# Reciprocal norms through TensorE to DRAM, first weight sums on VectorE, GpSimd multiplying before it splits: three moves in a one-core decoder block

## The chip, the cores and the metric

One core of a Trainium2 chip runs the whole block. The metric is device time in microseconds (us) of one execution, as a median over runs; all times in the sections on the profile come from one profiled execution. The engines are PE (TensorE), DVE (VectorE), ACT (ScalarE), POOL (GpSimd) and SP (SyncE, which issues most DMAs).

## The reference

One layer over 1024 tokens of width 1024, in float32, cut to what matters here:

```python
xn = rmsnorm(h, norm_mix_g)                 # row norms: y = x * rsqrt(mean(x*x) + eps)
proj = xn @ w_in                            # q, k, v, u, vg and one forget gate for each of 8 heads
att = forgetting_attention(q, k, v, log_sigmoid(proj[..., G_END:] + b_forget))
u, vg = gelu(proj_u), gelu(proj_vg)
mixed = einsum('gij,bnjgd->bnigd', tril(w_s), rmsnorm(vg)) + b_s     # 8 groups, chunks of 128
sg = u * mixed
h = h + concat([att, sg]) @ w_out
h = h + conv_ffn(rmsnorm(h)) @ ...          # w_up, causal convolution, silu gate, w_down
out = rmsnorm(h)
```

## The kernel before

Every float32 operand of a matmul is split into a high part (a cast to float32r) and a low part (the difference), and a product takes three matmuls: high by high, high by low, low by high. `tsplit` and `split_w` do this for weights (cast on ACT, difference on DVE, unless told otherwise); the result lies in a ring of six buffers (`wy`, `wy`, `whl` four times), so a cast waits until PE has read what the buffer held six splits ago. The projections are done as Strassen products over 2x2 blocks (in Winograd's form: sums S1 to S4 of weight blocks, T1 to T4 of x blocks).

The parts that the change touches, in the order of the program:

- **Row norms.** `rstd1` (128 x 8, token on the partition) holds the reciprocal norms. Products whose result has tokens on the partition use it as a per-partition scale. For k, whose result has tokens along the free axis, the norms must lie along the free axis on every partition: the kernel writes `rstd1` to DRAM (`rbd`, L411 to L413, a DMA on ACT's queue that stores 1024 single floats in transposed order) and reads it back broadcast into `rb` (L548, L549). `emit` multiplies k by `rb` (L625).
- **Weight sums of the q and k products.** `Weights(i)` loads four 128 x 512 blocks; `sums` and `last_sum` add them on POOL (L534, L537, L538, L544) for all four i. The sum S2 is then split, and its product is the third of the stage (`qk_step`). The products themselves are line L512: `q1` into bank `qc`, then `q2` into `qa`, then `qb`, `qc`, `qd`.
- **The forget gate.** The V products leave their last part in four PSUM banks `S2`. ACT copies 256 columns of each to SBUF (`copies`), and DVE adds 8 columns of each to `zf` (L562, recorded as L55). `q2` takes the first of these four banks, so its first matmul waits for both readers.
- **Gate normalisation.** `norm` multiplies half of the gated values by their reciprocal norms `gms` on DVE, 128 x 1024 at a time; `norm(1, 0)` and `norm(1, 2)` stand in front of the `zf` additions.
- **Spatial gating.** `spatial` runs eight groups g. The first half of the tokens is finished on DVE; of the second half ACT adds the bias into `t` and POOL multiplies `u[1]` by it (L808). PE then transposes both halves, `turn_sg(0, c)` and `turn_sg(1, c)` (L825), c from 0 to 3; the second needs POOL's products of groups 2c and 2c + 1.
- **Splits of the output weights.** `sg_split` splits four blocks `wrs`; for the first two the cast too is on POOL (L162), all four differences are (L166). They are used by `sg_out` (L1064 to L1066), which `fill` puts between the first attention logits (L976, L977) as filler for PE. DVE takes the row minimum of the logits (`logits_min`, L989).

ACT and DVE keep the order of the code in these stages (`Line` records it, and its operations have line L55 in the profile); where `on` is false, and for PE, POOL, SP and DMAs, a scheduler sets the order, with manual dependencies (`after`) for some.

## Time and profile before

| | |
|---|---|
| median of 3 runs | 1059.72 us (1059.09 to 1060.23) |
| profiled execution | 1062.91 us, of which the span of instructions is 1061.2 |
| PE busy | 1045.6 us, 99% of the span |
| DVE, ACT, POOL busy | 892.4, 564.7, 224.0 us |
| mean granted TensorE clock | 0.993 |
| HBM read and written | 115.68 and 45.05 MB |

Rows of a timeline give the start, the duration, the engine, the line, what is written and read, the count, and in brackets how long the engine was idle before and who ended that. Rows of a table by windows give, for each stretch, its length, then busy time and count for PE, PEld (weight loads), DVE, ACT and POOL, then the granted clock, the share of the DMA engines that was busy, and GB/s.

### The profile page before, as it was taken

How to read it: one execution, taken by the hardware profiler on the slowest of the kernel's cores; microseconds unless marked ns; L12 is line 12 of the kernel's file. 1: busy time of each engine (PE TensorE's matmuls, PEld its weight loads, DVE VectorE, ACT ScalarE, POOL GpSimd, SP SyncE). 2: the span in 40 equal slices, each digit the busy share in tenths (PEclk: the TensorE clock that was granted, in tenths of full speed). 3: DMA queues.
4: the chain of work that ended last, by engine and by line, in shares of the span. 5: the costliest groups of instructions: out<-in, count | busy, mean ns of one | idle time of the engine just before them, and what ended most of it. 6: DMA issues, size and time to landing. Idle time of an engine off the chain costs nothing.

```text
span 1061.2 us, 14270 instructions
## 1 busy us (share of the span) xinstructions
PE 1045.6 (99%) x4997; PEld 873.4 (82%) x4997; DVE 892.4 (84%) x1298; ACT 564.7 (53%) x1002; POOL 224.0 (21%) x169
## 2 busy tenths in 40 slices
PE   9999899989999999999999999999999999999997
PEld 6989788968888888888888888888888888888886
DVE  6897987858888869998999989989898866898775
ACT  6776533355777736654544444444444444544654
POOL 0001341220420740054333433323321000000000
PEclk9999999989999999999999999999999999999999
DMA  9624458848565445133245433332422899333442
GB/s 334 226 11 170 126 153 243 232 133 237 179 188 162 134 165 179 61 99 107 92 149 162 146 100 100 110 101 88 129 100 70 290 334 312 115 97 94 140 125 101
DMA packets 68475, 161.66 MB, mean 152 GB/s; under 512 B 9126, under 2 KB 10262, under 8 KB 68404
## 3 DMA queue, kind: packets, MB, share of 16 engines
q1 hardware_dynamic: 67092, 160.71, 48.0%
q8 instruction: 39, 0.64, 0.3%
q14 instruction: 32, 0.26, 0.1%
q10 hardware_dynamic: 1312, 0.04, 0.1%
HBM read 115.68 MB, written 45.05 MB: 151 GB/s over the span
## 4 chain that ended last, share of the span: by engine, by line
PE 82%; DVE 5%; ACT 3%; issue 1%; DMA 0%; POOL 0%; ACTq 0%; DVEq 0%; SPq 0%
PE k L1612 20%; PE qc L1352 11%; PE qd L1352 11%; PE qa L1352 10%; PE qb L1352 5%; PE pb L1040 3%; PE pb L1024 2%; PE qd L512 2%; PE qc L512 2%; PE qa L512 2%; PE ps L855 2%; PE pl L976 1%; PE pl L977 1%; PE pf L1064 1%; PE pf L1065 1%; PE pf L1066 1%
## 5 line engine op out<-in xcount | busy, mean ns | idle before, releaser
L1612 PE MATMUL k<-whb,wha 128*128 128x512 f32 (+1 forms) x936 | 209.9, 386 | 0.0
L1612 PEld LDWEIGHTS k<-whb,wha 128*128 128x128 f32 x936 | 174.1, 188 | 35.8 <-DVE wha L166 0.2
L1352 PE MATMUL qc<-xT,whb 128*128 128x512 f32 x540 | 129.9, 389 | 0.1
L1352 PE MATMUL qa<-xB,wha 128*128 128x512 f32 x528 | 127.4, 390 | 0.0
L1352 PEld LDWEIGHTS qc<-xT,whb 128*128 128x128 f32 x540 | 101.3, 188 | 21.6 <-ACT cg L1493 0.5
L1352 PEld LDWEIGHTS qa<-xB,wha 128*128 128x128 f32 x528 | 98.8, 188 | 20.8 <-DVE wha L166 0.4
L160 ACT CAST wha<-sg 128x512 fp32r<-128x512 f32 x77 | 47.8, 624 | 96.7 <-PE k L1612 84.1
L160 ACT CAST whb<-sg 128x512 fp32r<-128x512 f32 x82 | 50.7, 620 | 86.8 <-PE qc L1352 66.7
L166 DVE TENSOR_TENSOR wha<-sg,wha 128x512 fp32r<-128x512 f32 x77 | 52.8, 688 | 39.7 <-ACT wha L160 39.6
L1352 PE MATMUL qd<-xB,whb 128*128 128x512 f32 x264 | 63.7, 389 | 0.0
L1352 PE MATMUL qd<-xT,whb 128*128 128x512 f32 x264 | 63.7, 389 | 0.0
L1352 PE MATMUL qb<-xT,whb 128*128 128x512 f32 x252 | 61.0, 389 | 0.0
L166 DVE TENSOR_TENSOR whb<-sg,whb 128x512 fp32r<-128x512 f32 x82 | 57.0, 697 | 4.4 <-ACT whb L160 4.3
L1025 ACT CAST pt<-pb 128x512 fp32r<-128x512 f32 x72 | 40.6, 585 | 37.6 <-PE pb L1024 29.6
L1236 POOL TENSOR_TENSOR sg<-raw 128x512 f32<-128x512 f32 x20 | 31.1, 1553 | 139.7 <-DVE whb L166 79.9
L1352 PEld LDWEIGHTS qd<-xT,whb 128*128 128x128 f32 x264 | 49.5, 188 | 10.5 <-DVE u L1459 0.3
L1352 PEld LDWEIGHTS qd<-xB,whb 128*128 128x128 f32 x264 | 49.6, 188 | 10.3
L1026 DVE TENSOR_TENSOR pt<-pb,pt 128x512 fp32r<-128x512 f32 x72 | 47.3, 686 | 11.5 <-ACT pt L1025 11.2
L1352 PEld LDWEIGHTS qb<-xT,whb 128*128 128x128 f32 x252 | 47.2, 188 | 10.0 <-DVE whb L166 0.3
L1040 PE MATMUL pb<-pt,V 128*128 128x512 f32 (+3 forms) x192 | 49.6, 362 | 0.6 <-DVE pt L1026 0.6
L1239 POOL TENSOR_TENSOR sg<-sg,raw 128x512 f32<-128x512 f32 x20 | 33.3, 1663 | 63.5 <-DVE whb L166 63.5
L1237 POOL TENSOR_TENSOR sg<-sg,raw 128x512 f32<-128x512 f32 x20 | 35.1, 1756 | 47.2 <-issue 44.6
(409 smaller groups left out, 2259.8 us busy)
## 6 DMA issues: line engine op xcount, KB each, us to landing
raw<-wup SPq DMA_DIRECT2D x44, 512.0 KB
sg<-hx SPq DMA_DIRECT2D x77, 256.0 KB
hx<-hs SPq DMA_DIRECT2D x44, 256.0 KB
hx<-ca SPq DMA_DIRECT2D x35, 256.0 KB
xT<-wdn SPq DMA_DIRECT2D x28, 256.0 KB
x<-kd SPq DMA_DIRECT2D x24, 256.0 KB
A<-xtok SPq DMA_DIRECT2D x8, 512.0 KB
raw<-wqk SPq DMA_DIRECT2D x8, 512.0 KB
```

The costliest lines, as they stand in the source:

```text
L160: act.copy(h, src)
L166: return eng.tensor_tensor(out=l, in0=src, in1=f32(h), op=ALU.subtract)
L512: pe.matmul(ps, w[:, wi, ks], xs(n, xi, k), start=(first and c == 0), stop=(c == 11), skip_group_check=True)
L855: seq(pe.matmul(banks[m // 2][:, o:o + 256], xs(n, xi, 2 * j + kk)[:, ms], w[j][:, wi, kk * 256:kk * 256 + 256], start=(j == 0 and kk == 0 ...
L1025: casts.append(act.copy(pt[:, 0, :], ptr))
L1026: los.append(dve.tensor_tensor(out=pt[:, 1, :], in0=ptr, in1=f32(pt[:, 0, :]), op=ALU.subtract))
L1040: seq(pe.matmul(po[half][:, o:o + w], lhs, pt[:, s, c:c + w], start=(new and s == 0), stop=(s == 1 and (half, k) in ((1, 6), (0, 3))), ski ...
L1236: pool.tensor_tensor(out=s[0], in0=a21, in1=a22, op=ALU.add)
L1237: pool.tensor_tensor(out=s[1], in0=s[0], in1=a11, op=ALU.add)
L1239: pool.tensor_tensor(out=s[3], in0=s[1], in1=a12, op=ALU.add)
L1352: pe.matmul(ps, w[:, wi, ks], xb[:, xi, k, :], start=(first and n == 0), stop=(n == 11), skip_group_check=True)
L1612: pe.matmul((banks[bk + m] if ps is None else ps)[:, o], xh[:, xi, ms], wh[:, wi, o], start=((first and p_ == 0 or new) and n == 0), stop= ...
```

## The change

- `rstd1` is transposed by PE into unused columns of a PSUM bank, copied by ACT into the first 8 rows of `rb` (8 x 128), written to `rbd` as 8 rows of 128 floats by a DMA on SP's queue, and read back broadcast as before. The DMA on ACT's queue goes.
- For `Weights(0)` alone the four sums are done by DVE, between the splits; for i = 1, 2, 3 they stay on POOL.
- The split of S2 stands between `norm(1, 0)` and `norm(1, 2)`.
- POOL does the eight multiplications of `spatial` first, and then the splits of the output weights.

```diff
@@ after T4's products
-    act.on = False
-    act.dma_start(out=rbd.rearrange("a p -> p a"), in_=rstd1)
-    act.on = True
@@ before the products of S2's banks
+    pe.transpose(S[0][0:8, 384:512], rstd1, ident)
     S2 = [sbank() for _ in range(4)]
@@ class Weights
-        def sums(self, floor=None):
+        def sums(self, eng=pool, part=3):
...
+            if part & 2:
+                s2_ = sb("gg", [P, 512])
+                eng.tensor_tensor(out=a11, in0=a21, in1=a11, op=ALU.add)
+                eng.tensor_tensor(out=s2_, in0=a11, in1=a22, op=ALU.add)
+                self.src.update({"S3": a11, "S2": s2_})
+            if part & 1:
+                eng.tensor_tensor(out=a21, in0=a21, in1=a22, op=ALU.add)
+                self.src["S1"] = a21
...
     W = [Weights(0)]
-    rb = sb("t01", [P, 1024])
-    after(tc, sp.dma_start(out=rb, in_=rbd.rearrange("a b -> (a b)").unsqueeze(0).to_broadcast((P, 1024))), W[0].d)
     W[0].split("A11")
+    W[0].sums(dve, 2)
     act.activation(gms, gms, AF.Sqrt, bias=eps[:, 0:1], scale=1.0 / 64)
     dve.reciprocal(gms, gms)
     W[0].split("A12")
-    W[0].sums()
+    rb = sb("t01", [P, 1024])
+    act.copy(rb[0:8, 0:P], S[0][0:8, 384:512])
+    sp.dma_start(out=rbd, in_=rb[0:8, 0:P])
+    sp.dma_start(out=rb, in_=rbd.rearrange("a b -> (a b)").unsqueeze(0).to_broadcast((P, 1024)))
+    W[0].sums(dve, 1)
+    W[0].last_sum(dve)
     copies(S, vx[1], 1)
     norm(1, 0)
+    W[0].split("S2")
     norm(1, 2)
-    W[0].split("S2")
-    W[0].last_sum()
     copies(S2, vx[2])
@@ def sg_split
-        splits[:] = [split_w(wr, (w[:, 0], w[:, 1]), hi, "pool")]
+        if hi == "pool":
+            x = pool.tensor_copy(w[:, 0], wr)
+            after(tc, x, splits[0])
+            pool.tensor_tensor(out=w[:, 1], in0=wr, in1=f32(w[:, 0]), op=ALU.subtract)
+        else:
+            split_w(wr, (w[:, 0], w[:, 1]), hi, "pool")
@@ spatial, def second
-                x = pool.tensor_tensor(out=u[1], in0=v3(t), in1=u[1], op=ALU.mult)
-                after(tc, x, splits[0])
+                splits[:] = [pool.tensor_tensor(out=u[1], in0=v3(t), in1=u[1], op=ALU.mult)]
@@ ahead of spatial
-    for k in range(2):
-        whs.append(sg_split(wrs[k], "pool"))
@@ behind the first transposes
-    for k in range(2, 4):
-        whs.append(sg_split(wrs[k]))
+    for k in range(4):
+        whs.append(sg_split(wrs[k], "pool" if k < 2 else "act"))
```

DVE ahead of the gate additions, before: the splits of A11 and A12 (`whl` from `raw`), the two norms (`G` by `gms`), the split of S2 (`wy` from `gg`) and the first two additions to `zf`.

```order
L55 TENSOR_TENSOR whl_1065<-raw_1059,whl_1065 128x512
L55 RECIPROCAL gms<-gms 128x64
L55 TENSOR_TENSOR whl_1070<-raw_1059,whl_1070 128x512
L55 TENSOR_TENSOR G_187<-G_187,gms 128x1024 x2
L55 TENSOR_TENSOR wy_1089<-gg_1073,wy_1089 128x512
L55 TENSOR_TENSOR zf<-ps_1007,zf 128x8
L55 TENSOR_TENSOR zf<-ps_1008,zf 128x8
```

The same place on DVE after the change; `raw_1059` and `raw_1060` are the loaded weights, `gg_1066` is S2.

```order
L55 TENSOR_TENSOR whl_1063<-raw_1059,whl_1063 128x512
L55 TENSOR_TENSOR raw_1059<-raw_1060,raw_1059 128x512
L55 TENSOR_TENSOR gg_1066<-raw_1059,raw_1060 128x512
L55 RECIPROCAL gms<-gms 128x64
L55 TENSOR_TENSOR whl_1071<-raw_1059,whl_1071 128x512
L55 TENSOR_TENSOR raw_1060<-raw_1060 128x512
L55 TENSOR_TENSOR raw_1059<-gg_1066,raw_1059 128x512
L55 TENSOR_TENSOR G_187<-G_187,gms 128x1024
L55 TENSOR_TENSOR wy_1091<-gg_1066,wy_1091 128x512
L55 TENSOR_TENSOR G_187<-G_187,gms 128x1024
L55 TENSOR_TENSOR zf<-ps_1007,zf 128x8
L55 TENSOR_TENSOR zf<-ps_1008,zf 128x8
```

Four additions of 128 x 512 now stand on DVE in front of the `zf` additions, and one norm has moved behind the split of S2; the `zf` additions still stand behind both norms.

POOL around the spatial gating, before: `whl` from `raw` are the splits of the output weights, `A` from `pt` the multiplications.

```order
L846 TENSOR_TENSOR t_200_1733<-t_200_1733 72x128
L162 CAST whl_1934<-raw_1911 128x512
L162 CAST whl_1937<-raw_1911 128x512
L166 TENSOR_TENSOR whl_1934<-raw_1911,whl_1934 128x512
L166 TENSOR_TENSOR whl_1937<-raw_1911,whl_1937 128x512
L808 TENSOR_TENSOR A_189<-pt_1947,A_189 128x4x64 x4
L808 TENSOR_TENSOR A_189<-pt_1948,A_189 128x4x64 x4
L166 TENSOR_TENSOR whl_2044<-raw_1913,whl_2044 128x512
L166 TENSOR_TENSOR whl_2047<-raw_1913,whl_2047 128x512
```

The same place on POOL after the change.

```order
L852 TENSOR_TENSOR t_200_1735<-t_200_1735 72x128
L815 TENSOR_TENSOR A_189<-pt_1943,A_189 128x4x64 x4
L815 TENSOR_TENSOR A_189<-pt_1944,A_189 128x4x64 x4
L785 CAST whl_2040<-raw_1913 128x512
L785 CAST whl_2043<-raw_1913 128x512
L787 TENSOR_TENSOR whl_2040<-raw_1913,whl_2040 128x512
L787 TENSOR_TENSOR whl_2043<-raw_1913,whl_2043 128x512
L166 TENSOR_TENSOR whl_2046<-raw_1915,whl_2046 128x512
L166 TENSOR_TENSOR whl_2049<-raw_1915,whl_2049 128x512
```

Two casts and two differences have moved from in front of the eight multiplications to behind them, so that all four splits now stand in one row.

SP between the weight loads and the third weights' loads, after the change; `t` is `rb`, `vx` are stores of the V products. Before, the read of `rbd` stood between the loads of the first and the second weights, and the write was on ACT's queue.

```order
L520 DMA raw_1169<-wqk 128x1024
L580 DMA gg_1107<-bfv 128x8
L554 DMA rbd<-t_123_1074 8x128
L314 DMA vx<-wy_1080 128x1024
L555 DMA t_123_1074<-rbd 128x1024
L314 DMA vx<-whl_1095 128x1024
L519 DMA raw_1319<-wqk 128x1024
```

The write of the norms and their read now stand on SP's queue around the first store of V products.

More of the change, by code (lines that the diff above doesn't have):

```diff
@@ L528, in split, with last_sum @@
                 self.w[n] = tsplit(self.src[n])
-        def sums(self, floor=None):
+        def sums(self, eng=pool, part=3):
             a11, a21, a22 = self.a[:, 0, :], self.b[:, 0, :], self.b[:, 1, :]
-            s2_ = sb("gg", [P, 512])
-            x = pool.tensor_tensor(out=a11, in0=a21, in1=a11, op=ALU.add)
-            if floor is not None:
-                after(tc, x, floor)
-            pool.tensor_tensor(out=s2_, in0=a11, in1=a22, op=ALU.add)
-            pool.tensor_tensor(out=a21, in0=a21, in1=a22, op=ALU.add)
-            self.src.update({"S3": a11, "S2": s2_, "S1": a21})
-        def last_sum(self):
+            if part & 2:
[6 more added lines that the diff above has]
+                self.src["S1"] = a21
+        def last_sum(self, eng=pool):
             a12 = self.a[:, 1, :]
-            pool.tensor_tensor(out=a12, in0=self.src["S2"], in1=a12, op=ALU.add)
+            eng.tensor_tensor(out=a12, in0=self.src["S2"], in1=a12, op=ALU.add)
             self.src["S4"] = a12
     W = [Weights(0)]
-    rb = sb("t01", [P, 1024])
-    after(tc, sp.dma_start(out=rb, in_=rbd.rearrange("a b -> (a b)").unsqueeze(0).to_broadcast((P, 1024))), W[0].d)
     W[0].split("A11")
+    W[0].sums(dve, 2)
     act.activation(gms, gms, AF.Sqrt, bias=eps[:, 0:1], scale=1.0 / 64)
```

## The prediction

> **What bounds the kernel now.** I read the waits of PE first, because PE is busy 99% of the span. Each row gives who waited for whom, the total in us, how often, and the longest.

> ```profile
> PE qa L512 <- DVE zf L55: 2.8, 1, 2.8
> PE pb L825 <- POOL A L808: 2.1, 3, 0.7
> ```

> These are PE's two largest sums of waits, and the change touches the chains that end both: the `zf` additions on DVE, and the multiplications on POOL. Together they are only 5 us. The second view says that they cost more than themselves. It is the table by windows, in stretches of 3.41 us that I laid so that they meet the edges of the granted clock (after PEld, DVE, ACT and POOL the third number from the end is the clock):

> ```profile
> 107.54:110.95 3.41, 1.02 (x5) 0.52 (x3) 3.41 (x3) 0.00 (x0) 2.04 (x1) 1.00 0.46 183
> 213.34:216.76 3.42, 1.84 (x12) 1.12 (x12) 2.46 (x4) 3.42 (x8) 3.42 (x6) 1.00 0.75 235
> 216.76:220.17 3.41, 2.85 (x9) 2.46 (x10) 0.00 (x0) 1.35 (x3) 2.97 (x3) 0.50 1.02 234
> 223.58:227.00 3.42, 3.42 (x10) 2.64 (x8) 2.60 (x6) 2.17 (x4) 0.00 (x0) 0.50 0.00 1
> 233.83:237.24 3.41, 2.69 (x19) 2.12 (x18) 2.04 (x5) 1.16 (x4) 0.00 (x0) 1.00 0.30 95
> ```

> In the first two stretches PE is busy 30% and 54% of the time, and in the next one the clock is halved; after the second it stays so for three windows, to 227.00. The last row is a stretch with 79%, and behind it the clock stays full. So a wait of a few us on PE also slows what comes after it.

> **The first wait: what the change makes of it.** PE's timeline, and the chain's row for a product at full clock:

> ```profile
> 105.68 2.88 PE L512 MATMUL qc<-V,whl 128*128 128x512 f32 x12
> 111.40 4.38 PE L512 MATMUL qa<-x,whl 128*128 128x512 f32 x12 [2.84 <-DVE zf L55]
> 115.61 2.88 PE L512 MATMUL qb<-H,wy 128*128 128x512 f32 x12
> 115.78 2.72 PE qb L512 x12
> ```

> Twelve matmuls follow each other in 2.72 us. Without wait and clock loss `qb` would start at 105.68 + 2 x 2.72 = 111.12 in place of 115.61: 4.49 us are lost. PE gets one transpose more; the nearest row is that of the transposes of softmax sums, which have the same shape:

> ```profile
> L938 PE MATMUL pb<-ident,rs x8: 271/272/273, 246.1 to 371.5; 128*8 128x128 f32 x8
> ```

> That is 0.27 us with its latency, and I charge 0.15 (between 0 and 0.27). So up to 4.3 us are to be had, if the `zf` additions are done by 108.55. DVE before:

> ```profile
> 82.57 0.96 DVE L55 TENSOR_TENSOR G<-G 128x768 f32<-128x768 f32 x1 [1.74 <-DMA G<-wva]
> 85.62 0.43 DVE L55 TENSOR_TENSOR G<-gg,G 128x256 f32<-128x256 f32 x1 [2.09 <-DMA gg<-wvk]
> 102.23 0.69 DVE L55 TENSOR_TENSOR whl<-raw,whl 128x512 fp32r<-128x512 f32 x1
> 104.41 1.82 DVE L55 TENSOR_TENSOR whl<-raw,whl 128x512 fp32r<-128x512 f32 x1
> 106.15 4.51 DVE L55 TENSOR_TENSOR G<-G,gms 128x1024 f32<-128x1024 f32 x2
> 110.59 0.68 DVE L55 TENSOR_TENSOR wy<-gg,wy 128x512 fp32r<-128x512 f32 x1
> 111.19 0.37 DVE L55 TENSOR_TENSOR zf<-ps,zf 128x8 f32<-128x8 f32 x4
> 116.33 2.35 DVE L55 TENSOR_TENSOR G<-G,gms 128x1024 f32<-128x1024 f32 x2
> 107.34 2.24 POOL L544 TENSOR_TENSOR raw<-gg,raw 128x512 f32<-128x512 f32 x1
> ```

> The same instruction costs 0.69 (102.23) or 1.82 (104.41), and two norms 2.35 (116.33) or 4.51 (106.15); the dear ones lie beside POOL's sums. With POOL idle there, DVE does, from 102.23: the split of A11 0.60 (start to start, as 110.59 to 111.19), two sums 1.20, the reciprocal 0.25 (an estimate, from 0.55 beside POOL), the split of A12 0.60, two sums 1.20, a norm 1.18, the split of S2 0.60, a norm 1.18: 6.81, so `zf` begins at 109.04 and PE at 109.25, in place of 111.40. The four sums add 2.4 us to DVE, but the company of POOL that goes gives back 2.16 on the norms and 1.13 on the split. The moved split of S2 is in time for its product either way. So far 0.7 us of waiting would remain.

> The rest comes from the store of the norms. Its issue on ACT's queue, the issue on SP that waited for it to land, and the DMA's rate between the two and after:

> ```profile
> 67.12 0.39 ACTq L48 DMA_DIRECT2D rbd<-rstd  x1
> 79.30 0.39 SPq L549 DMA_DIRECT2D t<-rbd  x1
> 68.00:79.30 11.30, 11.30 (x51) 9.38 (x50) 11.30 (x17) 6.21 (x10) 0.00 (x0) 1.00 0.66 22
> 79.30:88.00 8.70, 8.70 (x40) 7.19 (x39) 4.87 (x9) 4.08 (x8) 0.00 (x0) 1.00 0.95 375
> ```

> For 12 us a store of 4 KB holds the DMA engines at 22 GB/s, and the V weights issued meanwhile wait behind it; that is DVE's idle 1.74 + 2.09 = 3.83 us at 82.57 and 85.62. With 8 rows of 512 bytes, at another time, these loads land before DVE asks for them. Not all of the 3.83 reaches `zf`, since the casts between write buffers that PE frees at its own pace; following the buffers through I get about 2 us, and 0.7 is enough. Bounds: nothing of it arrives, and the gain is 4.3 - 0.7 = 3.6; it arrives, and it is 4.3. I take **4.3**, as both ends lie close together and the idle time is in a row.

> The new road of the norms: PE's transpose lies 5 us ahead of ACT's copy of 8 x 128, which costs ACT a quarter of a us; SP's write waits for that copy with nothing late behind it (the next stores wait for ACT's later copies anyway), the read waits for the write, and behind it on SP the last store of V products and the third weights' loads wait. The rows are needed here:

> ```profile
> 124.99 1.24 DVE L625 TENSOR_TENSOR G<-G,t 128x512 f32<-128x512 f32 x1
> ```

> The copy comes at about 104.4 on the clock of before and some 2 us sooner after the change, so about 18 us lie between. I cost it at nothing; the price of its failing is the last rival.

> **The second wait.** PE's transposes of the two halves, and then the first logits after `sg_out`'s first tile; two neighbours give the step of a 512-wide matmul:

> ```profile
> 211.26 1.91 PE L825 MATMUL ps<-ident,A 128*128 128x128 f32 x16
> 213.21 0.66 PE L825 MATMUL pb<-ident,A 128*128 128x128 f32 x4
> 227.70 0.40 PE L976 MATMUL pl<-x 128*128 128x512 f32 x1
> 231.93 0.39 PE L1064 MATMUL pf<-whl,G 128*128 128x512 f32 x1
> 232.16 0.39 PE L1065 MATMUL pf<-whl,G 128*128 128x512 f32 x1
> 220.31 1.34 DVE L55 CUSTOM_DVE_ANT_0 t<-pl,t,lim 128x1024 f32<-128x1024 f32 x1 [4.34 <-PE pl L977]
> ```

> From 213.21 to 227.70 are 14.49 us. At full clock without waits for POOL: 16 transposes 1.91; the logits of row block 7, four steps of 0.23, 0.92; of block 6 (512 and 384 wide, by width) 0.80; then PE waits for the row minimum, since the third logits take the banks of the first: 1.34 of DVE less those 0.80, and 0.1 for the hand-over, 0.65; block 5 (512 and 256) 0.70; `sg_out` 12 x 0.23 = 2.76. Sum 7.74, so **6.75** are to be had. The wait of 0.65 is what is late next: in the slow clock it was nearly hidden. It leaves PE 81% busy in a window, more than the 79% that kept the clock.

> This needs POOL to be early with the multiplications, and not late with the splits:

> ```profile
> 207.55 1.36 POOL L162 CAST whl<-raw 128x512 fp32r<-128x512 f32 x2 [9.42 <-DMA raw<-wos]
> 211.75 5.52 POOL L808 TENSOR_TENSOR A<-pt,A 128x256 f32<-128x256 f32 x8
> L166 POOL TENSOR_TENSOR whl<-raw,whl 128x512 fp32r<-128x512 f32 x4 | 5.4, 1366 | 0.0
> 213.07 0.50 ACT L55 ACTIVATE pt<-pb,cp 128x256 f32<-128x256 f32 x1
> ```

> Each multiplication takes 0.69 (5.52 / 8) and follows ACT's bias; the last input is ready at 213.57, the last product at 214.3, and PE asks for it at 213.21 + 3 x 0.48 = 214.65. No wait. Then two casts (1.36) and four differences (4 x 1.37 = 5.48) end at 221.1, if nothing is earlier than before; ACT's last bias should be half a us sooner, since DVE's and POOL's work ahead of it no longer meet, so 220.6. `sg_out` wants the last of them at its eleventh matmul, 213.21 + 4.98 + 10 x 0.23 = 220.5. Just in time. DVE and the loads for later tiles move by less than their slack.

> **Sum.** 4.3 + 6.75 = 11.05. The profiled execution, 1062.91 with 1.7 outside its span of 1061.2, would become 1051.9. But it is 3.2 us above the median of the runs, and the one part of it that need not be the same in every run is the time at half clock; one window of 3.41 us more or less is 1.7. I take about 1 us off the gain for that and forecast a gain of 10.0: **1049.7 us** on the median of 1059.72. From 227.70 on PE hardly waits until the end, so nothing behind can eat what is won.

> **Rivals.** *The clock falls again in the second stretch.* Half the logits use 67 of 128 rows, and the half-clock window from 216.76 was 83% busy and still didn't bring the clock back; so a busy share may count for less there than I count it. Price: as before, three windows at half speed, 5.1 us; gain 11.05 - 5.1 = 6, 1053.7 us. Chance 0.18.

> *The splits are late on POOL.* Beside DVE an addition took POOL 2.24 (107.34). At that price the four differences take 9.0 in place of 5.5, and PE waits 3.6 us in the middle of `sg_out`, in place of the wait that is removed: 1049.7 + 3.6 = 1053.3. For it: they stand last in the row; against: DVE reads PSUM there, not two buffers in SBUF. Chance 0.12.

> *Only the waits go, since the clock drops were not theirs.* By my rows the drops follow windows of 30% and 54%; if they come in any case, the first stretch gives 2.84 - 0.15 = 2.7 and the second 6.75 - 5.1 = 1.65, together 4.35: 1055.4. Against it: three runs within 1.1 us don't look like drops that come by chance. Chance 0.04. [...]

> *Slower: the norms land too late.* The old store took 12.2 us (67.12 to 79.30). At the same price the new one, issued near 102.5, is done at 114.7 and read by 118, against a need at 124.99 - 4.3 = 120.7. Later than that DVE stands at L625 with the following splits behind it, and PE stands with it, 1 us for each after 2 us of slack; at 133 the whole gain is gone, and a landing at 138 would give about 1064. Against: 8 rows, not 1024 single floats. Chance 0.04. That nothing is changed at all, 0.02: the words "gate additions ahead of norms" are true of `norm(0, ...)` alone, where they stood ahead already.

> **How the numbers follow.** The forecast has 0.60 (its own range 1047.5 to 1051.5). The range takes in the rivals of the clock, of POOL and of the waits alone up to 1055.5, and below the full 11.05 with some of PE's later small waits, 1047.0. About 0.2% can be told from no change, 2.1 us; all cases but the last two gain more than that: faster 0.94, same 0.02, slower 0.04.

> **What would show it.** Right: no wait of `qa` for `zf` over 0.3 us and `qb` starting some 4.3 us sooner; no wait of L825's successor for POOL; granted clock 1.00 from 105 to 230; DVE not idle for `wva` and `wvk`; DMA above 300 GB/s soon after 70. Wrong: a stretch at 0.50, a wait of `pf` for `whl`, or of DVE's multiplication by `rb` for a DMA.

## The result and the profile after

The changed kernel takes 1052.78 us (1052.68 to 1052.88, 4 runs), the kernel before beside it on the same chip 1059.97 us (1059.09 to 1060.59): a ratio of 0.9933 (95% interval 0.9915 to 0.995), 7.2 us less where 10.0 were forecast. That lies inside the whole range, 1047.0 to 1055.5, but above the forecast's own, which ended at 1051.5. The profiled execution took 1052.88 us with a span of 1051.2; that of before had 1062.91 and 1061.2. So the profiles differ by 10.0 us, where 11.05 was added up, and the medians by 7.2. Of the 2.8 us that were missed, about 1.0 is missing in the profiles too; the other 1.8 is what the profiled run of before stood above its median beyond the 1 us taken off.

PE's waits after the change (who waited for whom, total us, times, longest), four of the largest behind the start of the program:

```profile
PE pb L1028 <- DVE raw L1071: 1.0, 2, 0.7
PE pb L1028 <- DVE pt L1030: 0.9, 1, 0.9
PE pl L980 <- DVE mn L55: 0.7, 1, 0.7
PE pl L980 <- DVE G L55: 0.4, 1, 0.4
```

Neither the wait of `qa` for `zf` nor the transposes' waits for POOL are left. PE's timeline at the two places:

```profile
105.91 2.93 PE L510 MATMUL qc<-V,whl 128*128 128x512 f32 x12
108.68 2.88 PE L510 MATMUL qa<-x,whl 128*128 128x512 f32 x12
111.40 2.88 PE L510 MATMUL qb<-H,wy 128*128 128x512 f32 x12
...
208.78 1.91 PE L831 MATMUL pb<-ident,A 128*128 128x128 f32 x16
211.09 0.50 PE L980 MATMUL pl<-x 128*128 128x512 f32 x1 [0.39 <-DVE G L55]
213.86 0.50 PE L980 MATMUL pl<-x 128*128 128x512 f32 x1 [0.74 <-DVE mn L55]
217.40 0.39 PE L980 MATMUL pl<-x 128*128 128x512 f32 x1
```

`qb` starts 4.21 us sooner (115.61 to 111.40). The second stretch, from the second half's transposes to the first logits behind `sg_out`'s first tile, takes 217.40 - 208.78 = 8.62 us in place of 14.49. DVE in front of the first place:

```profile
81.39 0.95 DVE L55 TENSOR_TENSOR G<-G 128x768 f32<-128x768 f32 x1
82.25 0.42 DVE L55 TENSOR_TENSOR G<-gg,G 128x256 f32<-128x256 f32 x1
99.87 0.69 DVE L55 TENSOR_TENSOR whl<-raw,whl 128x512 fp32r<-128x512 f32 x1
101.93 0.55 DVE L55 RECIPROCAL gms<-gms 128x64 f32<-128x64 f32 x1
104.14 1.22 DVE L55 TENSOR_TENSOR G<-G,gms 128x1024 f32<-128x1024 f32 x1
105.87 1.22 DVE L55 TENSOR_TENSOR G<-G,gms 128x1024 f32<-128x1024 f32 x1
107.01 0.37 DVE L55 TENSOR_TENSOR zf<-ps,zf 128x8 f32<-128x8 f32 x4
```

The two instructions that waited 3.83 us for `wva` and `wvk` have no bracket any more, each norm costs 1.22 us in place of 2.26, and `zf` is done 1.3 us before PE asks. The table by windows (length, then PE, PEld, DVE, ACT and POOL busy, clock, DMA share, GB/s): the DMA's rate where the old store lay, and PE in the second stretch, in windows of 3.41 us laid back from 1048.27, where this run's granted clock falls to 0.50 at its end.

```profile
67.00:79.00 12.00, 12.00 (x54) 9.95 (x53) 12.00 (x18) 6.88 (x11) 0.00 (x0) 1.00 0.48 179
208.59:212.00 3.41, 3.02 (x24) 2.65 (x23) 2.28 (x4) 3.41 (x9) 3.29 (x5) 1.00 0.83 262
212.00:215.41 3.41, 2.67 (x14) 2.01 (x13) 2.95 (x5) 2.32 (x5) 3.41 (x3) 1.00 1.02 213
```

179 GB/s in place of 22, and PE is busy 89% and 78% where it had 54%; the clock is 1.00 throughout. The norms' new road on SP, and POOL's end of the second stretch:

```profile
102.19 0.35 SPq L554 DMA_DIRECT2D rbd<-t  x1
103.81 0.42 SPq L555 DMA_DIRECT2D t<-rbd  x1
```

```profile
208.72 0.73 POOL L815 TENSOR_TENSOR A<-pt,A 128x256 f32<-128x256 f32 x1 [0.17 <-ACT pt L55]
209.39 1.17 POOL L785 CAST whl<-raw 128x512 fp32r<-128x512 f32 x2
210.52 2.52 POOL L787 TENSOR_TENSOR whl<-raw,whl 128x512 fp32r<-128x512 f32 x2
213.00 2.52 POOL L166 TENSOR_TENSOR whl<-raw,whl 128x512 fp32r<-128x512 f32 x2
```

The last product ends at 209.45, the splits at 215.52; `sg_out` asks for the last of them at 216.94.

### The profile page after: what moved, and what is told of

Its sections match the earlier page's. It is cut to its first block, busy times and chain, and to the rows that moved or that the text cites. A ratio compares the mean times of both kernels' runs of the same rounds, so it can differ in the third digit from the quotient of the medians.

```text
span 1051.2 us, 14265 instructions
## 1 busy us (share of the span) xinstructions
PE 1040.2 (99%) x4998; PEld 870.1 (83%) x4998; DVE 891.5 (85%) x1302; ACT 562.6 (54%) x1003; POOL 217.0 (21%) x165
## 4 chain that ended last, share of the span: by engine, by line
PE 96%; DVE 2%; ACT 1%; issue 0%; ACTq 0%; DVEq 0%
PE k L1616 20%; PE qc L1356 11%; PE qa L1356 11%; PE qd L1356 11%; PE qb L1356 5%; PE pb L270 5%; PE ps L270 5%; PE pb L1044 3%; PE pb L1028 2%; PE qc L510 2%; PE qd L510 2%; PE qa L510 2%; PE ps L861 2%; PE pl L980 1%; PE pf L1068 1%; PE pl L981 1%
## 5 line engine op out<-in xcount | busy, mean ns | idle before, releaser
L166 DVE TENSOR_TENSOR wha<-sg,wha 128x512 fp32r<-128x512 f32 x77 | 52.7, 687 | 37.1 <-ACT wha L160 36.9
L166 DVE TENSOR_TENSOR whb<-sg,whb 128x512 fp32r<-128x512 f32 x82 | 57.0, 697 | 4.4 <-ACT whb L160 4.3
L1030 DVE TENSOR_TENSOR pt<-pb,pt 128x512 fp32r<-128x512 f32 x72 | 47.3, 685 | 12.2 <-ACT pt L1029 11.9
```

What stands on the lines that cost most here:

```text
L166: return eng.tensor_tensor(out=l, in0=src, in1=f32(h), op=ALU.subtract)
L1030: los.append(dve.tensor_tensor(out=pt[:, 1, :], in0=ptr, in1=f32(pt[:, 0, :]), op=ALU.subtract))
```

## The experiments

The theory: the waits cost their own length in every run. They have a second price in the clock. In the profile of before the half clock lasts 3.41 us (110.95 to 114.36) and 10.24 us (216.76 to 227.00, three times as long), each time right behind a window of 3.41 us in which PE was busy for 30% and 54%. By the theory, my estimate from these rows, a wait halves the clock only where it leaves such a window too empty, and where the windows lie differs from run to run (near the first wait the half clock begins at 110.95 here, at 110.71 and 111.50 in two runs below). The profiled run of before then was among the unluckiest. The first rival: being profiled slowed that run's DMAs and made its waits longer. The second rival is the third of the prediction's own, that the half clock has nothing to do with the waits.

**The kernel before, once more**, with no edit.

> The kernel before, unchanged, profiled a second time: the whole change gave 10.0 us of span in the profiles and 7.2 us in the medians, and the difference is before's profiled execution, 3 us over its median. Theory W (the half-clock windows differ from run to run): the time stays at 1059.1 to 1060.6, and this profile has other half-clock stretches than 3.4 and 10.2 us, shorter by about 6 us in all (3 us of loss) if it comes out near 1060. Rival P (taking a profile slows something in before, such as the store of single floats with its 1024 packets): this profile is near 1063 again, with the same waits and the same stretches.

1059.73 us (1056.93 to 1061.6), 1.001 of before; the 31 runs of before beside it lie between 1056.28 and 1061.69. Its profiled run took 1058.61 us, span 1056.9. PE's timeline, and two of its windows:

```profile
107.11 2.88 PE L512 MATMUL qc<-V,whl 128*128 128x512 f32 x12
111.99 3.04 PE L512 MATMUL qa<-x,whl 128*128 128x512 f32 x12 [2.00 <-DVE zf L55]
```

```profile
108.32:111.73 3.41, 1.67 (x8) 1.05 (x6) 3.41 (x3) 0.00 (x0) 1.86 (x1) 1.00 0.40 157
214.13:217.54 3.41, 1.98 (x14) 1.46 (x13) 1.08 (x2) 2.82 (x7) 3.41 (x5) 1.00 1.01 297
```

The first wait is 2.00 us here and not 2.84, the three of 0.72 are unchanged, and no window between the start and the last 5 us is at half clock (its mean clock is 0.999, and one window of 3.41 us at half clock would take 0.0016 off): the emptiest of these two stretches have PE busy for 49% and 58%. It is the same kernel under the same profiler, so the first rival falls. From the start of `qc` to the end of the span this run takes 1056.9 - 107.11 = 949.8 us, the profile of the prediction 955.5, the changed kernel 945.3. At full clock the change is therefore worth 4.5 us; the other 5.7 of the first profile are half clock and the longer wait. The two places account for both. From `qc` to `qb` the three profiles take 7.76, 9.93 and 5.49 us; the second stretch takes 10.87 (212.54 to 223.41), 14.49 and 8.62.

**The norms' road alone** (the old store away; transpose, copy, 8-row write and read as in the change).

```diff
-    act.dma_start(out=rbd.rearrange("a p -> p a"), in_=rstd1)
+    pe.transpose(S[0][0:8, 384:512], rstd1, ident)
...
+    act.copy(rb[0:8, 0:P], S[0][0:8, 384:512])
+    sp.dma_start(out=rbd, in_=rb[0:8, 0:P])
```

> The new road of the norms alone; sums and POOL's order as before. Both theories: DVE's idle 3.8 us for the V weights goes, zf comes some 2 us sooner (109 in place of 111.2) and PE's wait for it falls from 2.8 to under 0.7 us, with no half clock behind it. Theory W: 2.7 to 4.3 us faster in the medians, about 1056 to 1057. Rival P, with the store as what the profile slows: under 2 us in the medians, about 1058 to 1059.

1055.94 us, 0.9977 (0.9966 to 0.9988). DVE's two norms, and PE's first wait:

```profile
104.09 4.56 DVE L55 TENSOR_TENSOR G<-G,gms 128x1024 f32<-128x1024 f32 x2
```

```profile
109.38 3.01 PE L510 MATMUL qa<-x,whl 128*128 128x512 f32 x12 [0.23 <-DVE zf L55]
```

The norms are as dear as before, beside POOL's sums, and yet the wait is nearly gone: the V weights that land in time are almost enough. DVE has no wait for them left: its additions of `wva` and `wvk` start at 81.23 and 82.10, without a pause.

**The VectorE sums alone** (`sums` and `last_sum` of `Weights(0)` on DVE, and the S2 split between the norms; the old store stays).

```diff
-    W[0].sums()
+    W[0].sums(dve, 1)
+    W[0].last_sum(dve)
     norm(1, 0)
+    W[0].split("S2")
     norm(1, 2)
```

> The VectorE sums alone: the norms keep their old road (128 x 8 stored transposed on ACT's queue) and GpSimd its old order. Theory (waits plus a clock whose windows fall differently in each run): with GpSimd idle the two norms cost 1.2 us each, but the loads of V weights are still late behind the store, so some 0.5 to 1 us of the first wait (2.0 us in the last profile of the kernel before) remains; the three waits of 0.72 us stay. 1058.2 us (1057 to 1059.5), some runs with a clock below 0.996. Rival (the first wait is due to the late loads alone, the four sums on VectorE eat what GpSimd's absence gives): wait unchanged at 2 us or longer, 1059 to 1060.

1056.48 us (1054.28 to 1059.94), 0.9971 (0.9959 to 0.9982): better than expected. DVE:

```profile
85.16 0.43 DVE L55 TENSOR_TENSOR G<-gg,G 128x256 f32<-128x256 f32 x1 [2.06 <-DMA gg<-wvk]
106.02 1.22 DVE L55 TENSOR_TENSOR G<-G,gms 128x1024 f32<-128x1024 f32 x1
108.89 0.38 DVE L55 TENSOR_TENSOR zf<-ps,zf 128x8 f32<-128x8 f32 x4
```

The loads are as late as ever, but the norms without POOL beside them bring `zf` to 108.89, and PE starts `qa` at 109.10 without a wait that the view lists. So this edit alone removes the first wait, and the norms' road alone leaves 0.23 us of it.

**GpSimd's order alone** (the eight products ahead of the splits).

```diff
-    for k in range(2):
-        whs.append(sg_split(wrs[k], "pool"))
...
-    for k in range(2, 4):
-        whs.append(sg_split(wrs[k]))
+    for k in range(4):
+        whs.append(sg_split(wrs[k], "pool" if k < 2 else "act"))
```

> POOL multiplies first, then splits; store and sums as before. Both theories: the three waits of 0.72 us behind the multiplications go, and from the first transposes to the end of the first filler tile some 8.6 us are left of 14.5, without half clock there; the wait for zf (2.8 us) stays. Theory W: 3 to 6 us faster in the medians, about 1054 to 1057. Rival P with the store: 5 to 6 us, 1054 to 1055.

1055.79 us (1054.26 to 1056.85), 0.9967 (0.9957 to 0.9978). The second stretch takes 221.03 - 212.39 = 8.64 us at full clock, the 8.6 expected. The first wait, 2.01 us as in the repeated profile of before, now has a half clock behind it. PE and its windows:

```profile
110.53 4.61 PE L512 MATMUL qa<-x,whl 128*128 128x512 f32 x12 [2.01 <-DVE zf L55]
```

```profile
107.30:110.71 3.41, 1.40 (x7) 0.86 (x6) 3.41 (x8) 0.23 (x2) 1.41 (x1) 1.00 0.38 154
110.71:114.12 3.41, 3.41 (x9) 2.63 (x10) 1.84 (x7) 3.24 (x7) 1.69 (x2) 0.50 0.01 5
```

A wait of the same length fell so that one window was 41% busy, not 49%, and the next ran at half clock.

**The norms' road and the VectorE sums together.** The edits of both.

> New road of the norms and VectorE sums, POOL's order around the multiplications as before. My accounting: the sums add nothing to e1 but the rest of the wait for zf, 0 to 0.7 us, so within 1 us of e1; the waits of 0.72 us and the half clock behind them stay. The rival that the sums carry the gain: e1 gains nothing and this one gains it all.

1058.33 us (1054.3 to 1060.24), 0.9988 (0.9973 to 1.0002): less of a gain than either alone. The first wait is gone, and the second stretch has become worse. POOL's first cast there, PE's first wait, two windows, and PE's last wait and the first logits behind `sg_out`'s first tile:

```profile
204.16 1.44 POOL L162 CAST whl<-raw 128x512 fp32r<-128x512 f32 x2 [10.68 <-DMA raw<-wos]
```

```profile
209.49 0.66 PE L827 MATMUL pb<-ident,A 128*128 128x128 f32 x4 [0.94 <-POOL A L810]
```

```profile
208.24:211.65 3.41, 1.63 (x11) 0.92 (x9) 2.58 (x4) 3.41 (x8) 3.41 (x6) 1.00 0.78 228
211.65:215.06 3.41, 2.57 (x10) 2.07 (x11) 0.00 (x0) 1.64 (x4) 3.41 (x5) 0.50 1.06 280
```

```profile
213.61 1.11 PE L827 MATMUL pb<-ident,A 128*128 128x128 f32 x4 [0.25 <-POOL A L810]
223.36 0.39 PE L978 MATMUL pl<-x 128*128 128x512 f32 x1
```

PE reaches this place 1.0 to 1.2 us sooner than with either edit alone, but POOL's cast waits for the output weights until 204.16 (204.13 with the norms' road alone). So PE waits four times, 2.63 us in all, a window is 48% busy, and three windows, to 221.88, run at half clock. Six of the ten runs (not seven, as an expectation below has it) have a mean clock of 0.994 or 0.995; with either edit alone it is one in ten and one in twelve.

**The kernel before, kept busy through the second waits.** Six more transposes of 0.12 us (1.91 / 16), overwritten at once, ahead of each transposition that waits.

```diff
-        pts.append(turn_sg(1, c, bank()))
+        pb1 = bank()
+        if c:
+            for _ in range(6):
+                seq(pe.transpose(pb1[:, 0:P], ut[1][:, 0, 0:P], ident))
+        pts.append(turn_sg(1, c, pb1))
```

> The kernel before with six more 128 x 128 transposes on TensorE (0.1 us each, results overwritten) ahead of each of the three transposes that wait for GpSimd, and nothing else: TensorE is busy through those waits, but the end of each wait stays where it is. Theory (TensorE's idleness in that stretch is what lets the clock halve, in the runs whose windows fall on it): no half clock between 205 and 240 us, the first wait and its own half clock stay; the runs above 1059.5 vanish, median 1057.5 us (1056.5 to 1058.5), against 1059.2. Rival (the clock falls for reasons of its own, and would fall after the change too): same spread as before, 1056.3 to 1061.7, and a median of 1059 to 1059.5.

1058.13 us (1055.68 to 1059.53) against 1059.71, 0.9986 (0.9976 to 0.9996): 1.6 of the expected 2.2 us. Its profile has no half clock in the second stretch, but neither had the repeated profile of before, and none of its 11 runs has a clock below 0.996, against 3 of 23 of before. The edit also changed something it was not meant to: behind the stretch DVE now does three additions of output tiles ahead of the last two row minima, where they stood between the two, and PE's transposes there no longer wait for DVE. From 223.47 to 233.53 PE takes 10.06 us, for work that took 11.45 in the repeated profile of before. That is 1.4 us without any half clock in either, so this run says little about the clock.

**The same on top of the two edits together.** 8, 6, 6 and 2 more transposes ahead of the four waits.

```diff
+        for _ in range((8, 6, 6, 2)[c]):
+            seq(pe.transpose(pb1[:, 0:P], ut[1][:, 0, 0:P], ident))
```

> The norms' new road and the VectorE sums together (1058.3 us before, with 7 of 10 runs at a clock of 0.994 or 0.995), and TensorE kept busy with 8, 6, 6 and 2 more transposes through its four waits for GpSimd in the second stretch (0.94, 0.72, 0.72 and 0.25 us). The waits end where they did. Theory (the two edits lost their gain there to the halved clock alone, since TensorE now waits 2.6 us in about 6 us and not 2.1): no half clock, every run at 0.997 or more, 1054.8 us (1054.2 to 1055.6). Rival (the two edits get in each other's way elsewhere): 1057.5 to 1058.5.

1053.58 us (1053.35 to 1054.94), 0.9941 (0.9925 to 0.9958), every run at a clock of 0.998 or more. PE computes nothing more that is used and waits for the same products, and the median is 4.75 us below that without the dummies (on another chip; by the ratios to before it is 5.0). The window at the place that was 48% busy, and PE's last wait and first logits as above:

```profile
208.78:212.19 3.41, 3.27 (x30) 3.04 (x29) 2.58 (x4) 3.41 (x9) 3.41 (x6) 1.00 0.67 227
```

```profile
213.68 0.66 PE L827 MATMUL pb<-ident,A 128*128 128x128 f32 x4 [0.22 <-POOL A L810]
220.41 0.39 PE L978 MATMUL pl<-x 128*128 128x512 f32 x1
```

The last transposes start at the same time, 213.61 and 213.68, and the same matmuls behind them take 9.75 us without the dummies and 6.73 with them: 3.0 us that are the clock's. Not all of the 4.75 is. Behind the stretch the order on DVE has changed as in the run before, and PE's transposes there, without the dummies and with them, are:

```profile
232.09 1.85 PE L1026 MATMUL pb<-ident,t 128*128 128x128 f32 x12 [0.72 <-DVE raw L1069]
```

```profile
227.82 1.94 PE L1026 MATMUL pb<-ident,t 128*128 128x128 f32 x16
```

That is worth 1.35 us (234.77 - 223.36 against 230.47 - 220.41) and has nothing to do with the clock. With 3.0 us in the same matmuls, and six of ten runs at 0.994 or 0.995 against none of five, the second rival has no ground left: the half clock is the waits' own.

**The changed kernel again.**

> The changed kernel again, for more runs beside the kernel before on one chip. Theory (without the idle windows the clock has nothing to fall on, in whatever phase its windows lie): all runs within 0.6 us, 1052.5 to 1053.1, clock 0.998 or more in each. Rival (its first four runs were lucky): about one run in three at 0.994 to 0.996 and 1054 to 1057 us, as in the kernel before.

1052.68 us (1052.46 to 1053.23, 5 runs), 0.9936 (0.9924 to 0.9948), with a clock of 0.998 to 1.000 in each; the 23 runs of before beside it spread over 5 us.

**Another order in the second stretch**, to win what was missed there.

```diff
-    for j in (7, 6):
+    for j in (6, 7):
...
+    sg_lo(1, 0, pts[0])
+    m6 = logits_min(0, 6, firsts[6])
+    sg_lo(1, 1, pts[1])
+    fill((-1, 5))
+    m7 = logits_min(0, 7, firsts[7])
```

> The changed kernel with another order at the second stretch: the low parts of the first transposed group ahead of the row minima, logits of row block 6 before those of 7, and the first output tile of the spatial gating ahead of the logits of row block 5, so that TensorE has work while VectorE takes the row minimum. Theory (what was missed of the second stretch are the waits of 0.39 us for the low parts and 0.74 us for the row minimum, each worth its own length, since TensorE is the bound to the end): up to 1.1 us less than the changed kernel, 1051.7 us (1051.3 to 1052.6; the last split on GpSimd may now be 0.2 us late). Rival (the stretch ends with VectorE's or ACT's exponentials anyway, later waits give it back): 1052.7.

1053.51 us (1052.5 to 1054.3), 0.9941 (0.9929 to 0.9954): no gain; at 0.8 us above the changed kernel on the same chip it is nearer to the rival. PE's second and third wait in the stretch:

```profile
216.48 0.50 PE L1071 MATMUL pf<-whl,G 128*128 128x512 f32 x1 [0.16 <-POOL whl L166]
219.10 0.50 PE L980 MATMUL pl<-x 128*128 128x512 f32 x1 [0.54 <-DVE mn L55]
```

With the first, 0.39 us as in the changed kernel, they sum to 1.09 us, where the changed kernel has 0.39 + 0.74 = 1.13. The wait for the row minimum moved to a later row block, and the POOL wait came in. Why the median is higher by 0.8 stays open.

**The first wait put back, long.** In the changed kernel the S2 difference is done six times more on DVE ahead of the second norm.

```diff
     W[0].split("S2")
+    for _ in range(6):
+        dve.tensor_tensor(out=W[0].w["S2"][:, 1], in0=W[0].src["S2"], in1=f32(W[0].w["S2"][:, 0]), op=ALU.subtract)
     norm(1, 2)
```

> The changed kernel with the difference of the S2 split done seven times over in place of once on VectorE (six times 0.6 us more in front of the gate additions; same values): the gate additions begin near 110.6 us, TensorE needs them at 108.7 us. Theory (a wait of about 2 us costs itself, and in about half of the runs, those whose clock windows fall on it, half a window of 1.7 us more): first wait 1.9 to 2.2 us, runs from 1054.6 to 1056.6 us, median 1055.5 us, some profiles with a stretch at 0.50 of 3.41 us. [...]

1060.17 us (1059.67 to 1062.98), 1.0006 (0.9991 to 1.0022). The delay was mis-set: POOL's sums of the next weights came to lie beside the last repeats, which took 1.3 us each. DVE, PE and two windows:

```profile
108.01 4.02 DVE L55 TENSOR_TENSOR wy<-gg,wy 128x512 fp32r<-128x512 f32 x3
```

```profile
113.39 5.29 PE L510 MATMUL qa<-x,whl 128*128 128x512 f32 x12 [5.20 <-DVE zf L55]
```

```profile
108.09:111.50 3.41, 0.11 (x1) 0.00 (x0) 3.34 (x4) 0.00 (x0) 3.23 (x2) 1.00 0.05 18
111.50:114.91 3.41, 1.52 (x4) 1.26 (x5) 2.97 (x11) 1.05 (x3) 0.00 (x0) 0.50 0.01 2
```

A wait of 5.20 us costs 7.4 on the median: two windows at half clock follow, and all 11 runs have a clock of 0.997 or less, where the nine of the changed kernel have 0.998 or more.

**The first wait put back, shorter.** One difference of A12 and three of S2 too many.

```diff
+    for _ in range(1):
+        dve.tensor_tensor(out=W[0].w["A12"][:, 1], in0=W[0].src["A12"], in1=f32(W[0].w["A12"][:, 0]), op=ALU.subtract)
...
+    for _ in range(3):
+        dve.tensor_tensor(out=W[0].w["S2"][:, 1], in0=W[0].src["S2"], in1=f32(W[0].w["S2"][:, 0]), op=ALU.subtract)
```

> The changed kernel with four differences too many on VectorE in front of the gate additions (one for A12, three for S2; same values), after six of them cost a wait of 5.2 us, half clock of 6.8 us behind it, and 7.5 us in all. The scheduler puts one more split among them, and the last ones lie beside GpSimd: the gate additions should begin near 111 us and TensorE wait 2.0 to 3.0 us, as long as in the kernel before. Theory (a wait of that length fills more than half of a clock window in some positions of the windows and not in others): runs of two kinds, 1055 to 1055.6 us where the clock stays full and 1056.5 to 1057.5 us where it is halved for one window, median 1056.2 us. [...]

1056.31 us (1055.77 to 1056.88, 6 runs), 0.9969 (0.9956 to 0.9981). The median is the theory's, but two kinds of run can't be told apart in a spread of 1.1 us, and the changed kernel's 1052.7 and the 2.94 us of waiting that its profile has are 1055.6: inconclusive by its times. The two slowest have a clock of 0.998 and the four others 0.999, so at most two can have had a half clock. If half busy were the edge (behind 48% the clock halved, behind 49% it did not, but behind 54% it did), a wait of 2.94 us would halve it, by estimate from these lengths, in all but 0.5 us of the 3.41 us of positions that it can have against the windows. So how often such a wait costs the clock stays open. The profile shows a run in which it did not, with the wait across the edge of two windows:

```profile
112.21 2.97 PE L510 MATMUL qa<-x,whl 128*128 128x512 f32 x12 [2.94 <-DVE zf L55]
```

```profile
107.09:110.50 3.41, 2.19 (x10) 1.46 (x8) 3.34 (x6) 0.79 (x2) 1.23 (x1) 1.00 0.65 243
110.50:113.91 3.41, 1.70 (x8) 1.44 (x9) 3.34 (x9) 0.16 (x1) 2.55 (x2) 1.00 0.01 2
```

2.94 us of waiting, 64% and 50% busy, and the clock stays full; 2.84 us in the prediction's profile left one window 30% busy, and the clock halved.

## Why the prediction was right, and where its size was off

- **The first wait: right against the profile that it was read from.** 4.3 us forecast, 4.21 in the profiles. DVE's split of A11 starts 6.04 us ahead of `qc` (99.87 against 105.91) in place of 3.45 (102.23 against 105.68): the loads gave 2.6 us (2 estimated). DVE's row from A11's split to `zf` took 7.14 us (6.81): the reciprocal costs 0.46 from start to start without POOL too, not 0.25, and the first two sums follow each other at 0.72. But DVE was late in the prediction's profile: the repeated profile of before has 4.30 in place of 3.45, and a wait of 2.00 us; the two other runs with this part unchanged have waits of 2.01 and 1.8. Against these the loads gave 1.7 us. That the size came out to 0.1 us is owed to measuring against the same late profile. That is also why the lower bound, with 0.7 us of waiting left, was too careful: in the run with the sums alone DVE starts 4.38 us ahead of `qc`, and no wait is left.
- **The second wait: right in kind, 0.88 us too much.** 6.75 us forecast, 14.49 - 8.62 = 5.87 in the profiles. The step that failed is the sum of 7.74: it left out the wait for the low parts (0.39), put the row minimum at 0.65 (0.74), and counted the logits of three row blocks 0.4 us too short: the first matmul behind a wait takes 0.34 us to the next (from 211.09 and from 213.86), not 0.23, and the last ahead of a wait runs its full length, 0.34 (from 212.78).
- **POOL: right, with more room.** No wait for its products or its splits; the differences took 1.26 us each, not 1.37, and the last split had 1.4 us to spare, not none.
- **The norms' road: right at nothing.** Written at 102.19, read from 103.81; its first use, DVE's multiplication at L627, starts at 121.08, and no wait for that DMA is listed. The slower rival had no ground.
- **The clock as a price of waits: right.** The changed kernel has full clock at both places; its window with the row minimum was 78% busy (81% worked out) and kept it.
- **The mis-sized term: what the half clock is worth in a median run.** The prediction's own rows split its 11.05 into 4.35 for waits alone (the third rival's sum) and 6.7 for the clock, of which "about 1 us" was taken off. The full-clock profiles put the waits at 4.5, so by estimate about 2.7 of the 7.2 are the clock's, where 5.7 were kept. The step that failed is that deduction: the profiled run stood 3.2 us above the median, three runs of before lay within 1.1 us, and I read that as a clock that falls in every run. The longer series (31 runs, 1056.28 to 1061.69) spread over 5 us at mean clocks from 0.994 to 0.999, and the repeated profile has none of the 13.65 us at half clock that the first has between its start and its last 5 us. Taking off all 3.2 gives 7.85. That the time still fell inside the whole range is owed to the room left for rivals, and none of them happened.
- **The rivals.** The times of the first two, 1053.7 and 1053.3, lie nearest to the measured one, but neither happened: no stretch at half clock, no wait for POOL's splits. The third was right on the waits' own worth and wrong on the cause. The wait of 2.01 us had a half-clock window behind it and the wait of 5.20 us two, and filling gaps of 0.94 us and less brought back 3.0 us in the same matmuls. The wait of 2.94 us alone, across the edge of two windows, left the clock at 1.00.

What stays open is how the 7.2 us of the medians divide between waits and clock: 4.5 and 2.7 rest on one profile of before at full clock. The kernel kept busy on the second waits alone (1058.13) can't tell, since 1.4 us of its gain lie elsewhere and its first wait kept a half clock.

## What to carry to other kernels

Before a stall is priced from one profile, set that run's time against the spread of many runs: what it stands above the median is the first thing to take off a gain read from it. Here four waits of 2.63 us in all on a busy TensorE went with 10.23 us at half clock, and the matmuls behind them took 3.0 us more than with the gaps filled; with an earlier stretch repaired PE had come there 1.0 to 1.2 us sooner than with either edit alone, so that repair made this stretch worse until it was repaired too. Such edits have to be tried together. Filling work that is meant to change one stretch can move another, so compare such a run with its base stage by stage, not by its total alone. Here DMA moved 22 GB/s while a store of 1024 single floats lasted (68.00 to 79.30), and DVE waited 3.83 us for another queue's loads; with the norms transposed first and stored as 8 rows, their read was issued 1.62 us behind the write (102.19, 103.81), and no wait for it is listed.
